# Five of the six sections of adaptive weights move from TensorE to ScalarE and GpSimd

## The chip, the cores and the metric

The kernel runs on one core of a Trainium2 chip. The metric is the device time of one execution in microseconds (us), the median of several runs. The engines of the core, as the profile names them, are PE (TensorE matmul) with PEld (its weight loads), DVE (VectorE), ACT (ScalarE), POOL (GpSimd) and SP (SyncE, which issues nearly all DMAs here). Each engine works off its own queue strictly in order.

## The reference

The program runs two blocks of a network over 256 tokens of width 1024, in float32. The first block has two layers, each steered by vectors that are computed from one conditioning vector `c`:

```python
silu_c = jax.nn.silu(c)                       # (1, 1024)
for i in range(DEPTH):                        # 2 layers
    mod = silu_c @ ada_w[i] + ada_b[i]        # (1, 6 * 1024)
    sh_t, sc_t, ga_t, sh_c, sc_c, ga_c = jnp.split(mod, 6, axis=-1)
    hn = modulate(rms_norm(x, norm_tm_g[i]), sh_t, sc_t)
    tm = rwkv7_mix(hn, ...) if i % 2 == 0 else dilated_attention_mix(hn, ...)
    x = x + ga_t[:, None, :] * tm
    ...                                       # mixture of experts, steered by sh_c, sc_c, ga_c
```

The change concerns `silu_c @ ada_w[i]` alone: a row of 1024 numbers times a 1024 x 6144 matrix, for two layers. The work that runs beside it is `rwkv7_mix` of layer 0, a recurrence over the tokens in two directions.

## The kernel before

The 2 x 6144 columns are cut into six sections of 2048 columns, one `Ada.steps(i, s)` each. A section reads 8 MB of weights in eight tiles of 1 MB, `[128 partitions, 2048 columns]`; partition p of tile k holds row 8 p + k of the matrix. TensorE takes a tile as the moving operand, in four column blocks j of 512, and `c[:, k]` (spread over 32 columns) as the weights, so that the four blocks land in four groups of 32 partitions of one PSUM bank. The eight k accumulate there. VectorE then adds the bias, and writes the section into the tiles `R`.

Section one is needed at once. The other five are a generator, `side`, that `rwkv` runs beside its own work; it yields after every k:

- `weave(preps(1, ...), every(side, 2))`: the second half of the preparation of the recurrence (decays, keys, scaled by VectorE, ScalarE and GpSimd). `kknorm` begins it; it sums squares on PE (L871), takes the root on ACT (L873) and goes on from there.
- `weave(inverses(), every(side, 2))`: the inverses of 16 x 16 triangular blocks, thirty dependent VectorE instructions (L1008, L1010) on `mcm`, which GpSimd clears first (L996, L998), transposed at the end by PE (L1015) and copied by ACT (L1017).
- `roundrobin([chain(0), chain(1), every(side, 3)])`: the recurrence, here called the chain. There are 16 jobs, eight in each direction, two at a time; a job starts with L1114 on PE, L1120 to L1124 on DVE and the transposition L1138 on PE, and ends with `across` (L1221 to L1241).

`every(gen, n)` lets n more turns pass after each step of `gen`. The final order on each engine is set by the tile scheduler, which merges the streams, so program order is only where it starts from.

Weight tiles come from a pool of four slots of 1 MB. In this stage some slots are held by others: `lb` until the last L894, `G` (a norm weight) during sections whose index s is 0 or 2, and `lg2` during the chain. A DMA into a slot waits until the last reader of the tile before is done.

Of the kernel before, what the change touches and what calls it, by code (L numbers as in the profile page):

```python
# [20 lines left out]
F32 = mybir.dt.float32  # L21
F32R = mybir.dt.float32r
I32 = mybir.dt.int32
AF = mybir.ActivationFunctionType
OP = mybir.AluOpType
AX = mybir.AxisListType
P = 128
# [3 lines left out]
KD = 8  # L31
# [550 lines left out]
def weave(main, *fill, rest=True):  # L582

    fill = [iter(f) for f in fill]
    for _ in main:
        while fill:
            try:
                next(fill[0])
                break
            except StopIteration:  # L590
                fill.pop(0)
    for f in fill if rest else ():
        finish(f)


def every(gen, n):

    for _ in gen:
        for _ in range(n):
            yield  # L600
# [104 lines left out]
def rwkv(N, src, I, cst, emit, side, tail, scratch):  # L705


    nc, tc = N.nc, N.tc
# [105 lines left out]
    def into_v(n):  # L814
# [4 lines left out]
            else:  # L819
                sc.activation(o, ps, AF.Copy)  # L820
        return ev
    side = iter(side)
    xk = shift_split(1, True)
    proj_fm(N, sp, *xk, wk, 0, into_fm(kf, 0))
    load_constants()
# [19 lines left out]
    ps = N.psum("b")  # L845
# [149 lines left out]
    def inverses():  # L995
        g.memset(mcm, 0.0)  # L996
        for c in range(16):
            g.memset(mcm[:, c, :, c:c + 1], 1.0)  # L998
        for t4 in range(4):
            ps = N.psum("b")  # L1000
            for t in range(4):
                nc.tensor.transpose(ps[0:64, t * P:(t + 1) * P], nd[:, 4 * t4 + t, :], N.ident)
            sc.activation(ncm[:, 4 * t4:4 * t4 + 4].rearrange("p t b i -> p (t b i)"), ps[0:64, :], AF.Copy)
        yield
        for k in range(15, 0, -1):
            n = 16 - k
            tv = tmp[:, 0:n * 8 * k].rearrange("p (c b i) -> p c b i", c=n, b=8)
            v.tensor_mul(tv, ncm[:, k:k + 1, :, 0:k].to_broadcast([64, n, 8, k]),  # L1008
                         mcm[:, k:, :, k:k + 1].to_broadcast([64, n, 8, k]))
            v.tensor_add(mcm[:, k:, :, 0:k], mcm[:, k:, :, 0:k], tv)  # L1010
            yield
        for h in range(2):
            ps = N.psum("b")
            for c in range(8):
                nc.tensor.transpose(ps[:, c * 64:(c + 1) * 64], mcm[:, 8 * h + c].rearrange("p b i -> p (b i)"),  # L1015
                                    N.ident[0:64, 0:64])
            sc.activation(m16[:, 8 * h:8 * h + 8], ps.rearrange("p (c x) -> p c x", c=8), AF.Copy)  # L1017
    m16 = pool("m16", 1, eM, "left").tile([P, 16, 64], F32, name="m16")
    weave(inverses(), every(side, 2), rest=False)
    e2s.close()  # L1020
    en.close()

# [223 lines left out]
    def chain(buf, jobs):  # L1246
        for z, et in jobs:
            yield from job(z, et, buf)
    late = []
    gens = [chain(0, [(0, et) for et in range(8)]), chain(1, [(1, et) for et in range(8)]), every(side, 3)]  # L1250
    roundrobin(gens)
    e4s.close()
    eM.close()
# [548 lines left out]
class Ada:  # L1802
# [34 lines left out]
    def steps(self, i, s):  # L1837
        N, I = self.N, self.I
        nc = N.nc
        v = nc.vector  # L1840
        S = self.np_.tile([P, 512], F32, name=N.nm("S"), tag="gt")
        b = I["ada_b"]
        nc.gpsimd.dma_start(S, bass.AP(tensor=b.tensor, offset=b.offset + i * 6144 + s * 2048,
                                       ap=[[512, 4], [0, 32], [1, 512]]))
        if s in (0, 2):
            gn = I["norm_tm_g" if s == 0 else "norm_cm_g"]
            h = slice(64, 128) if s == 0 else slice(0, 64)
            G = N.wp.tile([P, 2048], F32, name=N.nm("G"), tag="w")[:, 0:512]
            nc.gpsimd.dma_start(G[h], bass.AP(tensor=gn.tensor, offset=gn.offset + i * D, ap=[[512, 2], [0, 32], [1, 512]]))
        ps = N.psum("b")  # L1850
        w = I["ada_w"][i].rearrange("(p k) n -> p k n", k=KD)
        for k in range(KD):
            wt = N.wload(w[:, k, s * 2048:(s + 1) * 2048])
            for j in range(4):
                nc.tensor.matmul(ps[32 * j:32 * j + 32, :], self.c[:, k:k + 1].to_broadcast([P, 32]),  # L1855
                                 wt[:, j * 512:(j + 1) * 512], start=k == 0, stop=k == KD - 1)
            yield
        v.tensor_add(S, S, ps)
        if s in (0, 2):
            v.scalar_tensor_tensor(S[h], S[h], 1.0, G[h], op0=OP.add, op1=OP.mult)  # L1860
        q = 3 * i + s
        for k, r in enumerate(self.R):
            v.scalar_tensor_tensor(r, S, self.row[:, q:q + 1], r.bitcast(F32), op0=OP.mult, op1=OP.add)
            if k == 0:
                v.tensor_sub(S, S, r.bitcast(F32))
        yield
# [83 lines left out]
class Model:  # L1950
# [3 lines left out]
    def all(self):  # L1954
# [5 lines left out]
        with ExitStack() as es:  # L1960
# [28 lines left out]
            for i in range(2):  # L1989
                cm = {}  # L1990

                def emit(tt, n, ps):
                    xs = x[:, tt, HALVES[n]]
                    t = np_.tile([P, 512], F32, name=N.nm("gt"), tag="gt")
                    v.tensor_mul(t, ps, cm["ga"][n])
                    v.tensor_add(xs, xs, t)
                    cm["rms"].add(tt, n, xs, ps)
                    if n:
                        modulated(N, cm["rms"], tt, [x[:, tt, h] for h in HALVES], cm["A"], cm["B"], cm["h"][:, tt])

                if i == 0:
                    def side():
                        for q in range(1, 6):
                            yield from ada.steps(q // 3, q % 3)
                    mixer = rwkv(N, src, I, I["cst_rwkv"], emit, side(), tail, lambda k: half("G", k))
                else:
                    mixer = dilated(N, src, I, I["cst_attn"], emit, tail)
                next(mixer)
                cm["ga"] = gate(i, 2, "c")
                if i == 0:  # L2010
                    late = es.enter_context(tc.tile_pool(name="late", bufs=1))
                moe = Moe(N, I["moe_router_g"][i], I["moe_router_g_b"][i], I["moe_router_e"][i], I["moe_router_e_b"][i], True,
                          f(I["moe_w_gate"][i]), f(I["moe_w_up"][i]), f(I["moe_w_down"][i]))
                cm["rms"] = Rms(N, np_)
                cm["h"] = moe.xg_tile().rearrange("q k (t p) -> q t k p", t=NT)
                cm["B"], cm["A"] = ([ada.part(i, m, n, "c") for n in range(2)] for m in (3, 4))
                finish(mixer)
                N.open_extra(NEXTRA[1] + 2)
                moe.open()
                for tt in range(NT):  # L2020
                    moe.take(tt, cm["h"][:, tt])
                moe.scale = gate(i, 5)
                moe.route()
                nx = {}
                w = I["at_w_qkv"][0]

                def following(nx=nx, w=w):
                    AB = N.wtile("AB", own=True)
                    for j, (m, nm) in enumerate(((0, "B"), (1, "A"))):
                        nx[nm] = AB[:, j * D:(j + 1) * D]  # L2030
                        for n, h in enumerate(HALVES):
                            sc.activation(nx[nm][:, h], ada.part(1, m, n), AF.Copy)
                    N.prefetch(proj_srcs(w, 2048) + proj_srcs(w, 0)[:1], own=True)
                if i:
                    fg = halves("R")
                    for n, h in enumerate(HALVES):
                        nc.sync.dma_start(fg[n], I["final_g"][h].partition_broadcast(P))
                    ca = causal_setup(N, late)
                acc = moe.run(x, end=following if i == 0 else lambda: N.prefetch(mix_first(I, 0), own=True))
                rms = Rms(N, np_)  # L2040
                if i == 0:
                    def setup(tile, nx=nx):
                        nx["h"] = [tile(), tile()]

                    def norm(tt, acc=acc, rms=rms, nx=nx):
                        for n, h in enumerate(HALVES):
                            rms.add(tt, n, acc[tt, n], x[:, tt, h])
                        hk = nx["h"][tt].rearrange("q (k p) -> q k p", k=KD)
                        modulated(N, rms, tt, [acc[tt, n] for n in range(2)], *([nx[a][:, h] for h in HALVES] for a in "AB"), hk)
                        for n, h in enumerate(HALVES):  # L2050
                            sc.activation(x[:, tt, h], acc[tt, n], AF.Copy)
                    src = Source(norm, lambda tt, k, nx=nx: nx["h"][tt][:, k * P:(k + 1) * P], setup)
# [141 lines left out]
```

## Time and profile before

| what | us |
|---|---|
| median of 3 runs (2389.83 to 2395.27) | 2390.19 |
| the profiled execution, its own time | 2402.28 |
| its span in the trace | 2400.5 |
| PE busy / DVE busy / ACT busy / POOL busy | 2077.4 / 1154.3 / 707.3 / 366.4 |
| matmuls of the six sections (L1855), busy | 86.1 |

The span is the time between the first and the last instruction of the profiled execution. Busy times are unions over an engine's instructions; a PE that is busy need not be at its peak, since matmuls are pipelined and their ends are modelled. Idle time of an engine is written with what ended it. In this kernel the stretch that matters lies between 145 and 507 us of the span: 145 to 245 us preparation, 245 to 277 us inverses and the start of the first job, 277 to 507 us the chain.

### The profile page before, as it was taken

How to read it: one execution, taken by the hardware profiler on the slowest of the kernel's cores; microseconds unless marked ns; L12 is line 12 of the kernel's file. 1: busy time of each engine (PE TensorE's matmuls, PEld its weight loads, DVE VectorE, ACT ScalarE, POOL GpSimd, SP SyncE). 2: the span in 40 equal slices, each digit the busy share in tenths (PEclk: the TensorE clock that was granted, in tenths of full speed). 3: DMA queues.
4: the chain of work that ended last, by engine and by line, in shares of the span. 5: the costliest groups of instructions: out<-in, count | busy, mean ns of one | idle time of the engine just before them, and what ended most of it. 6: DMA issues, size and time to landing. Idle time of an engine off the chain costs nothing. (4 is left out here: it accounts for less than half of the span.)

```text
span 2400.5 us, 39938 instructions
## 1 busy us (share of the span) xinstructions
PE 2077.4 (87%) x16032; PEld 1482.2 (62%) x16032; DVE 1154.3 (48%) x2599; ACT 707.3 (29%) x1277; POOL 366.4 (15%) x300
## 2 busy tenths in 40 slices
PE   4987799897987799998997799989897799979895
PEld 2864366665653498997654377766564577766552
DVE  4777778774321435347331266563231575652132
ACT  2432244342110344434110234531120245421120
POOL 1144102231000221211000112220010222210010
PEclk7986799888998899999998899989998899989998
DMA  8424533156999663436999844477999544569996
GB/s 273 141 93 143 204 111 136 59 215 257 405 419 419 224 208 106 160 121 240 383 417 419 322 151 132 149 255 307 418 408 413 184 136 140 173 266 402 413 406 271
DMA packets 162994, 606.00 MB, mean 252 GB/s; under 512 B 36960, under 2 KB 37984, under 8 KB 107488
## 3 DMA queue, kind: packets, MB, share of 16 engines
q1 hardware_dynamic: 159072, 599.64, 65.9%
q0 software_dynamic: 3136, 3.16, 0.5%
q8 instruction: 132, 2.16, 0.4%
q10 hardware_dynamic: 576, 0.39, 0.1%
q14 instruction: 78, 0.64, 0.1%
HBM read 602.09 MB, written 1.05 MB: 251 GB/s over the span
## 5 line engine op out<-in xcount | busy, mean ns | idle before, releaser
L360 PE MATMUL psb<-w,xg 128*32 128x256 f32 (+1 forms) x4096 | 390.2, 427 | 88.4 <-DMA w<-in_moe_w_gate_dram 26.7
L360 PEld LDWEIGHTS psb<-w,xg 128*32 128x32 f32 (+1 forms) x4096 | 213.1, 133 | 274.0 <-issue 64.3
L562 ACT ACTIVATE wh<-w 128x1024 fp32r<-128x1024 f32 x230 | 240.6, 1060 | 291.1 <-PE psb L652 157.7
L566 POOL TENSOR_TENSOR wl<-w,wh 128x1024 fp32r<-128x1024 f32 x80 | 198.5, 2483 | 586.5 <-ACT wh L562 449.4
L566 DVE TENSOR_TENSOR wl<-w,wh 128x1024 fp32r<-128x1024 f32 x150 | 200.5, 1343 | 169.8 <-ACT wh L562 140.0
L420 DVE SCALAR_TENSOR_TENSOR hid<-psb,gs,sg 128x256 f32<-128x256 f32 x44 | 30.0, 682 | 394.4 <-PE psb L360 394.4
L651 PE MATMUL psb<-wh,xh 128*128 128x512 f32 x448 | 185.4, 415 | 4.0 <-ACT wh L562 2.4
L652 PE MATMUL psb<-wh,xl 128*128 128x512 f32 x448 | 181.5, 406 | 0.3 <-DVE xl L143 0.3
L360 PE MATMUL psb<-w,hT 128*32 128x512 f32 (+1 forms) x1024 | 173.3, 609 | 8.4 <-DMA w<-in_moe_w_down_dram 3.9
L649 PE MATMUL psb<-wl,xh 128*128 128x512 f32 x448 | 132.2, 403 | 3.2 <-POOL wl L566 1.7
L142 ACT ACTIVATE yh<-psb 128x512 fp32r<-128x512 f32 x88 | 52.5, 597 | 234.6 <-DVE psb L441 130.1
L1855 PE MATMUL psb<-w,c_fm 128*32 128x512 f32 x384 | 86.1, 779 | 35.1 <-DMA w<-in_ada_w_dram 29.5
L143 DVE TENSOR_TENSOR yl<-psb,yh 128x512 fp32r<-128x512 f32 x88 | 60.9, 692 | 104.7 <-ACT yh L142 104.7
L360 PEld LDWEIGHTS psb<-w,hT 128*32 128x32 f32 (+1 forms) x1024 | 50.7, 121 | 97.1 <-issue 70.8
L360 PE MATMUL psb<-pm,xh 128*128 128x256 f32 (+1 forms) x384 | 102.0, 302 | 4.3 <-DVE pm L343 3.2
L651 PEld LDWEIGHTS psb<-wh,xh 128*128 128x128 f32 x448 | 86.8, 194 | 24.3 <-ACT wh L562 3.6
L649 PEld LDWEIGHTS psb<-wl,xh 128*128 128x128 f32 x448 | 86.1, 194 | 23.4 <-POOL wl L566 2.5
L404 ACT ACTIVATE pt<-psb 128x256 fp32r<-128x256 f32 x44 | 16.9, 385 | 282.0 <-PE psb L360 282.0
L360 PE MATMUL psb<-pm,xl 128*128 128x256 f32 (+1 forms) x384 | 98.4, 292 | 0.0
L652 PEld LDWEIGHTS psb<-wh,xl 128*128 128x128 f32 x448 | 87.0, 194 | 18.4 <-DVE xl L143 1.2
L620 PE MATMUL psb<-axh,wh 128*128 128x256 f32 x384 | 93.7, 282 | 0.0
L620 PE MATMUL psb<-axl,wh 128*128 128x256 f32 x384 | 93.7, 282 | 0.0
(582 smaller groups left out, 3889.1 us busy)
## 6 DMA issues: line engine op xcount, KB each, us to landing
w<-in_moe_w_gate_dram SPq DMA_DIRECT2D x64, 1024.0 KB, 18.7
w<-in_moe_w_up_dram SPq DMA_DIRECT2D x64, 1024.0 KB, 18.5
w<-in_moe_w_down_dram SPq DMA_DIRECT2D x64, 1024.0 KB, 19.8
w<-in_w_exp_up_dram SPq DMA_DIRECT2D x64, 1024.0 KB, 13.2
w<-in_w_exp_gate_dram SPq DMA_DIRECT2D x64, 1024.0 KB, 10.3
w<-in_w_exp_down_dram SPq DMA_DIRECT2D x64, 1024.0 KB, 15.8
w<-in_ada_w_dram SPq DMA_DIRECT2D x48, 1024.0 KB, 5.1
w<-in_w_in_dram SPq DMA_DIRECT2D x44, 1024.0 KB, 5.1
```

Source lines behind the costliest of these rows:

```text
L142: self.nc.scalar.activation(hi, src, AF.Copy)
L143: (eng or self.nc.vector).tensor_sub(lo, src, hi.bitcast(F32))
L360: keep(nc.tensor.matmul(*a, **k))
L404: nc.scalar.activation(pt[g], ps[:, 0:256], AF.Copy)
L420: v.scalar_tensor_tensor(hid[g].rearrange("s j p -> s p j"), pu[:, :256].rearrange("s (p j) -> s p j", j=2), gs[g], sg.rearrange("s (p j) ...
L562: nc.scalar.activation(wh, w, AF.Copy)
L566: i = (nc.gpsimd if eng == "g" else nc.vector).tensor_sub(wl, w, wh.bitcast(F32))
L620: mm = lambda a, b, **f: nc.tensor.matmul(o, a[:, kk, ws], b[:, k, :], skip_group_check=True, **f)
L649: nc.tensor.matmul(pss[tt], xh[:, k, t], wl[:, kk, :], start=False, stop=k == nk - 1)
L651: nc.tensor.matmul(pss[tt], xh[:, k, t], wh[:, kk, :], start=k == 0, stop=False)
L652: nc.tensor.matmul(pss[tt], xl[:, k, t], wh[:, kk, :], start=False, stop=False)
L1855: nc.tensor.matmul(ps[32 * j:32 * j + 32, :], self.c[:, k:k + 1].to_broadcast([P, 32]), wt[:, j * 512:(j + 1) * 512], start=k == 0, stop=k ...
```

## The change

Section one stays as it was. In sections two to six a weight tile is now `[128, 4, 512]`: four k of one column block j. ScalarE multiplies each block of 512 columns in place by its per-partition number `c[:, k]`, GpSimd adds the eight products up into a tile `asum` in SBUF (seven additions), and TensorE sums `asum` over the partitions with one matmul against ones per j. The generator yields after two k, four times per column block, and no longer passes through `every`; the next weight tile is requested one ahead (`N.prefetch`). The new tile `asum` lies in the recurrence's pool `rp`, which is why `side` is now called with it.

```diff
-    side = iter(side)
+    side = iter(side(rp))
...
-    weave(inverses(), every(side, 2), rest=False)
+    weave(inverses(), side, rest=False)
...
-    gens = [chain(0, [(0, et) for et in range(8)]), chain(1, [(1, et) for et in range(8)]), every(side, 3)]
+    gens = [chain(0, [(0, et) for et in range(8)]), chain(1, [(1, et) for et in range(8)]), side]
...
-        for k in range(KD):
-            wt = N.wload(w[:, k, s * 2048:(s + 1) * 2048])
+        if i == s == 0:
+            for k in range(KD):
+                wt = N.wload(w[:, k, s * 2048:(s + 1) * 2048])
+                for j in range(4):
+                    nc.tensor.matmul(ps[32 * j:32 * j + 32, :], self.c[:, k:k + 1].to_broadcast([P, 32]),
+                                     wt[:, j * 512:(j + 1) * 512], start=k == 0, stop=k == KD - 1)
+                yield
+        else:
+            g = nc.gpsimd
+            srcs = [w[:, 4 * n:4 * n + 4, s * 2048 + j * 512:s * 2048 + (j + 1) * 512] for j in range(4) for n in range(2)]
             for j in range(4):
-                nc.tensor.matmul(ps[32 * j:32 * j + 32, :], self.c[:, k:k + 1].to_broadcast([P, 32]),
-                                 wt[:, j * 512:(j + 1) * 512], start=k == 0, stop=k == KD - 1)
-            yield
+                a = self.sums.tile([P, 512], F32, name=N.nm("asum"), tag="asum")
+                for k in range(KD):
+                    if k % 4 == 0:
+                        wt = N.wload(srcs[2 * j + k // 4])
+                        if k or j < 3:
+                            N.prefetch(srcs[2 * j + k // 4 + 1:][:1])
+                    u = wt[:, k % 4]
+                    sc.activation(u, u, AF.Copy, scale=self.c[:, k:k + 1])
+                    if k == 1:
+                        g.tensor_add(a, wt[:, 0], u)
+                    elif k:
+                        g.tensor_add(a, a, u)
+                    if k % 2:
+                        yield
+                nc.tensor.matmul(ps[32 * j:32 * j + 32, :], N.ones.bitcast(F32).to_broadcast([P, 32]), a, start=True, stop=True)
```

Counted over five sections: 160 matmuls go (two records each in the trace), 20 matmuls, 160 ScalarE instructions and 140 GpSimd instructions come; the 40 MB of weights are the same.

Three places in the queues show where the scheduler put the new work. The rows name line, operation, output<-input with buffer numbers, and shape; line numbers of the change are those of the changed kernel (L1870 the scaling, L1872 and L1874 the additions, L1877 the matmul with ones).

First, POOL at the end of the preparation, before: the last products `bk` of the preparation (L932), the clearing of `mcm` for the inverses, and the first job's `DP` stand together.

```order
L932 TENSOR_TENSOR bk_1403<-cu_1476,sg_1480 128x512
L912 COPY pl_836<-E_1551 128x8
L918 TENSOR_TENSOR ar_1402<-rf,E_1551 128x512
L932 TENSOR_TENSOR bk_1405<-cu_1485,sg_1489 128x512
L932 TENSOR_TENSOR bk_1404<-cu_1540,sg_1544 128x512
L932 TENSOR_TENSOR bk_1406<-cu_1549,sg_1553 128x512
L996 MEMSET mcm 64x2048
```

The same place of the change:

```order
L1872 TENSOR_TENSOR asum_1818<-w_1803 128x512
L1874 TENSOR_TENSOR asum_1818<-asum_1818,w_1803 128x512 x2
L1874 TENSOR_TENSOR asum_1818<-asum_1818,w_1830 128x512 x4
L932 TENSOR_TENSOR bk_1404<-cu_1538,sg_1542 128x512
L932 TENSOR_TENSOR bk_1406<-cu_1547,sg_1551 128x512
L1872 TENSOR_TENSOR asum_1856<-w_1857 128x512
L1874 TENSOR_TENSOR asum_1856<-asum_1856,w_1857 128x512 x2
L1874 TENSOR_TENSOR asum_1856<-asum_1856,w_1859 128x512 x2
L996 MEMSET mcm 64x2048
```

Between `aa_1499` (the last L901 but one of the preparation) and the clearing of `mcm` POOL now has 26 additions; 23 more follow up to the end of section three (`asum_2134`), which makes 49.

Second, PE around the first job's transposition L1138, before: it stands behind one matmul of section four.

```order
L1114 MATMUL psb_1968<-ar_839,bk_843 64x128 x2
L1855 MATMUL psb_1998<-w_1999,c_fm 32x512 [waits DMAHW5_49,DVE_49,PE_49]
L1855 MATMUL psb_1998<-w_1999,c_fm 32x512 x3
L1138 MATMUL psc_2010<-ident,MQB_1917 128x128 [waits DVE_49]
L1138 MATMUL psc_2010<-ident,MQB_1917 128x128 x3
```

In the change it stands behind the sum over the last column block of section three, which waits for GpSimd:

```order
L1114 MATMUL psb_2001<-ar_839,bk_843 64x128 [waits DVE_49,PE_49]
L1114 MATMUL psb_2001<-ar_839,bk_843 64x128 x7
L1877 MATMUL psb_1855<-asum_2134,ones 32x512 [waits Pool_49]
L1138 MATMUL psc_2036<-ident,MQB_1950 128x128 [waits DVE_49]
L1138 MATMUL psc_2036<-ident,MQB_1950 128x128 x3
```

So the first job cannot pass L1138 until GpSimd has finished all of section three.

Third, ACT before the root of `kknorm` (L873), before:

```order
L908 ACTIVATE sg_1284<-cu_1280 128x512 [waits Activation_49]
L820 ACTIVATE vt<-psb_1195 128x512 [waits PE_49]
L873 ACT_TABLE_LOAD
L873 ACTIVATE ri_1432<-psb_1427 8x256 [waits PE_49]
L897 ACT_TABLE_LOAD [waits PE_49]
```

The same place of the change has sixteen of the twenty scalings that now stand ahead of the root:

```order
L820 ACTIVATE vt<-psb_1195 128x512 [waits PE_49]
L1870 ACTIVATE w_1424<-w_1424,c_fm 128x512
L1870 ACTIVATE w_1492<-w_1492,c_fm 128x512 [waits DMAHW6_49,Pool_49]
L1870 ACTIVATE w_1492<-w_1492,c_fm 128x512 x3
L1870 ACTIVATE w_1600<-w_1600,c_fm 128x512 [waits DMAHW7_49,Pool_49]
L1870 ACTIVATE w_1600<-w_1600,c_fm 128x512 x3
L1870 ACTIVATE w_1695<-w_1695,c_fm 128x512 [waits DMAHW0_49,Pool_49]
L1870 ACTIVATE w_1695<-w_1695,c_fm 128x512 x3
L873 ACT_TABLE_LOAD
L873 ACTIVATE ri_1434<-psb_1429 8x256 [waits PE_49]
```

## Rows read from the trace of the kernel before

**Rows 1.** Page, busy us, share of the span and instructions of each engine.
```profile
PE 2077.4 (87%) x16032; PEld 1482.2 (62%) x16032; DVE 1154.3 (48%) x2599; ACT 707.3 (29%) x1277; POOL 366.4 (15%) x300
```

**Rows 2.** Windows: stretch, length, busy us of PE, PEld, DVE, ACT, POOL, clock, DMA.
```profile
205.00:245.00 40.00, 27.03 (x231) 17.29 (x234) 35.05 (x68) 8.18 (x17) 17.52 (x33) 0.66 0.38 127
245.00:277.00 32.00, 17.05 (x140) 6.37 (x132) 26.64 (x47) 1.20 (x2) 6.20 (x8) 0.68 0.73 258
277.00:507.00 230.00, 213.79 (x3367) 155.36 (x3367) 167.53 (x459) 95.23 (x275) 45.98 (x74) 0.95 0.32 109
```

**Rows 3.** The same windows, of L1855 alone: busy us of PE and PEld.
```profile
145.00:205.00 60.00, 10.20 (x36) 1.58 (x36) 0.74 0.35 123
277.00:507.00 230.00, 39.54 (x184) 5.52 (x184) 0.95 0.32 109
```

**Rows 4.** Timeline of PE, 225 to 300 us: start, us, instruction, idle before and releaser.
```profile
263.45 1.94 PE L1855 MATMUL psb<-w,c_fm 128*32 128x512 f32 x8 [3.15 <-DMA w<-in_ada_w_dram]
265.32 1.86 PE L1015 MATMUL psb<-ident,mcm 64*128 64x64 f32 x15
...
274.43 1.93 PE L1855 MATMUL psb<-w,c_fm 128*32 128x512 f32 x8 [3.83 <-issue]
277.02 1.12 PE L1138 MATMUL psc<-ident,MQB 128*128 128x128 f32 x4 [0.65 <-DVE MQB L1124]
...
287.66 1.04 PE L1855 MATMUL psb<-w,c_fm 128*32 128x512 f32 x2
```

**Rows 5.** Timeline of POOL, 180 to 300 us.
```profile
206.54 1.61 POOL L918 TENSOR_TENSOR ar<-rf,E 128x512 f32<-128x512 f32 x1
208.12 1.81 POOL L901 TENSOR_SCALAR aa<-aa 128x512 f32<-128x512 f32 x2
...
213.52 1.17 POOL L918 TENSOR_TENSOR ar<-rf,E 128x512 f32<-128x512 f32 x1
214.67 1.25 POOL L932 TENSOR_TENSOR bk<-cu,sg 128x512 f32<-128x512 f32 x1
...
216.09 1.17 POOL L918 TENSOR_TENSOR ar<-rf,E 128x512 f32<-128x512 f32 x1
```

**Rows 6.** Timeline of DVE, 180 to 300 us.
```profile
206.44 0.68 DVE L915 TENSOR_TENSOR ar<-kn,E 128x512 f32<-128x512 f32 x1
207.04 1.66 DVE L917 TENSOR_TENSOR bk<-bk,sg 128x512 f32<-128x512 f32 x1
...
213.42 3.99 DVE L929 TENSOR_SCALAR cu<-aa,pv 128x256 f32<-128x256 f32 x2
...
245.00 0.28 DVE L1008 TENSOR_TENSOR tmp<-ncm,mcm 64x120 f32<-64x120 f32 x1 [1.99 <-ACT ncm L1003]
...
261.65 0.35 DVE L1010 TENSOR_TENSOR mcm<-mcm,tmp 64x120 f32<-64x120 f32 x1
```

**Rows 7.** Timeline of ACT, 180 to 300 us.
```profile
188.63 0.37 ACT L873 ACTIVATE ri<-psb 8x256 f32<-8x256 f32 x1 [16.38 <-PE psb L871]
```

**Rows 8.** Groups of instructions, 120 to 240 us (ACT) and 277 to 507 us (others).
```profile
L908 ACT ACTIVATE sg<-cu 128x512 f32<-128x512 f32 x8 | 5.0, 622 | 0.0
L1078 POOL TENSOR_TENSOR G<-G,lw 128x512 f32<-128x512 f32 x6 | 7.6, 1269 | 0.6 <-DMA lw<-in_rw_ln_b_dram 0.2
L1124 DVE TENSOR_TENSOR MQB<-m,cm 128x512 f32<-128x512 f32 x15 | 16.0, 1095 | 5.0 <-PE psb L1187 5.0
L1130 DVE TENSOR_TENSOR bk<-bk,pl 128x256 f32<-128x256 f32 x16 | 8.1, 504 | 2.5 <-PE psb L1114 2.5
```

**Rows 9.** Waits, 277 to 507 us: who waited for whom, us in total, times, longest.
```profile
DVE ZZ L1151 <- PE psb L1149: 20.2, 17, 3.1
DVE MQB L1172 <- PE psb L1169: 18.0, 22, 1.8
```

**Rows 10.** DMA issues by line: KB each, median us from issue to landing.
```profile
w<-in_ada_w_dram SPq DMA_DIRECT2D x48, 1024.0 KB, 5.1
w<-in_rw_w_rkv_dram SPq DMA_DIRECT2D x12, 1024.0 KB, 5.7
```

More of the change, by code (lines that the diff above doesn't have):

```diff
@@ L1839, in steps @@
         nc = N.nc
-        v = nc.vector
+        v, sc = nc.vector, nc.scalar
         S = self.np_.tile([P, 512], F32, name=N.nm("S"), tag="gt")
@@ L2001, in all, with side @@
                 if i == 0:
-                    def side():
+                    def side(pool):
+                        ada.sums = pool
                         for q in range(1, 6):
                             yield from ada.steps(q // 3, q % 3)
-                    mixer = rwkv(N, src, I, I["cst_rwkv"], emit, side(), tail, lambda k: half("G", k))
+                    mixer = rwkv(N, src, I, I["cst_rwkv"], emit, side, tail, lambda k: half("G", k))
                 else:
```

## The prediction

> **What bounds the kernel now.** The first view is the table of engines. PE is busy 2077.4 of 2400.5 us (87%), POOL 366.4 (15%) [rows 1]. That is an average; the five sections run between 145 and 507 us, so the next view is the same table by stretch [rows 2]. Three stretches have different limits.
>
> From 205 to 245 us, the end of the preparation, DVE is busy 35.05 of 40 us and PE 27.03. From 245 to 277 us, the inverses, DVE has 26.64 of 32 and PE 17.05. In neither is PE the limit: DVE is, with POOL (17.52 of the first 40 us) feeding it. From 277 to 507 us, the chain, PE is busy 213.79 of 230 us (93%), DVE 167.53, ACT 95.23 and POOL 45.98. The list of waits of this stretch has DVE waiting for PE at the top, 20.2 us at L1151 and 18.0 us at L1172 [rows 9]. So PE leads there, though a recurrence also has a chain of its own, DVE to PE and back.
>
> L1855 costs PE 39.54 us in the chain (184 records) and 10.20 us between 145 and 205 us [rows 3]. The change can therefore give something back in the chain; in the stretches ahead of it TensorE has idle time, and VectorE and GpSimd, to which it adds, have the dependent work.
>
> **The prices.** A scaling on ACT has the shape of L908, 622 ns; an addition on POOL that of L1078, 1269 ns (one SBUF operand overwritten, the other from a weight tile) [rows 8]. A sum over the partitions, one column block alone in two records, took 1.04 us at full clock [rows 4]. The DMA of a weight tile with shorter rows is that of `in_rw_w_rkv`, 5.7 us instead of 5.1 [rows 10]: no difference by itself. Over five sections that is 160 x 0.62 = 99 us of ACT, 140 x 1.27 = 178 us of POOL, 20 x 1.04 = 21 us of PE.
>
> **(a) Preparation.** Before `kknorm`, PE no longer runs L1855 in 145 to 205 us. If all of it lay on the path that would be 10.2 us, if none, nothing; PE is not full there, and I take 4 us. Twenty scalings, 20 x 0.62 = 12.4 us, now stand ahead of the root L873 on ACT. They lie in the 16.38 us for which ACT idled there before, waiting for PE [rows 7], and so cost nothing; if a weight tile lands late or a slot comes free late, everything behind the root (`ri`, then the keys) moves by what is missing, up to 12 us.
>
> **(b) The start of the chain.** This is the largest term. The first job's transposition L1138 began at 277.02 us [rows 4]. In the change it stands on PE behind the sum over `asum_2134`, and PE works in order; so it cannot begin before POOL has done 49 additions that come after `aa_1499`. Before, `aa_1499` (the first of the two L901 at 208.12) ended at about 209.0 us [rows 5]; 4 us earlier by (a), 205. What else POOL does up to the chain is 17.52 + 6.20 us [rows 2], less the L918 of 1.61 and the half of L901 of 0.9 that are over by 209.0 [rows 5]: 21 us.
>
> The price of an addition beside DVE is not shown in the trace of before. Below, it is 1.27 us: 205 + 21 + 49 x 1.27 = 288, or +11 us. Above, it alternates each time with one DVE instruction of about the 0.68 us of L915 [rows 6], making 1.9: 205 + 21 + 93 = 319, or +42. The trace does show that the two engines hold each other up: L917 on DVE took 1.66 us beside POOL's L918, where L915, of the same shape and kind, took 0.68 [rows 6], and L929, two instructions, took 3.99 us during three POOL operations [rows 5, 6]. On the other side POOL's L918 took 1.61 us in that company and 1.17 us elsewhere [rows 5]. DVE is 83 to 88% busy here [rows 2], but a part of its work reads PSUM or one SBUF tile; I take half of the additions as meeting such an instruction, 1.55 us each: 205 + 21 + 76 = 302, **+25 us**.
>
> The Trainium skill, page "SBUF — State Buffer", section "Who interferes with whom", says that VectorE and GpSimd share a port pair under an exclusive lock, and that a VectorE operation with two SBUF inputs and a GpSimd operation that reads SBUF fully block each other. The trace agrees as far as L917's 1.66 against 0.68 us goes. By the rule taken to the full the sum would use the upper 319 us.
>
> DVE pays as well. The clearing of `mcm`, which opens the inverses (first L1008 at 245.00 us, last L1010 at 261.65 [rows 6]), is behind 26 of the 49 additions: 205 + 26 x 1.55 = 245, plus POOL's other work up to there, 21 less the 6.20 after 245 us, 15, is 260. The thirty short dependent instructions then take turns with additions: 16.65 us become at most 16.65 + 23 x 1.27 = 46. From 260 that ends between 277 and 306, so this second path arrives no later than the first by more than 4 us, and I count it once.
>
> **(c) The chain.** PE loses 39.54 us [rows 3] and gets 12 sums back, 12.5 us: 27 us less, 187 of some 225. ACT gets 96 scalings (60 us, to 155), POOL 84 additions (107 us, to 153) [rows 2, 8]; none of them is full. The gain lies between nothing and 27 us; as PE is 93% busy and DVE waits for it, nearer the upper end: 16 us. Against it, DVE's L1124 (1095 ns) and L1130 (504 ns) [rows 8] have two SBUF inputs and will meet additions: 16 jobs, at most one addition of 1.2 us each, 0 to 19 us; I take 8. Each sum makes PE wait for POOL's last addition, with the jobs' matmuls queued behind; 12 sums, at most one addition late each, 0 to 15 us. A tile is held for its DMA (5.7), four scalings (2.5) and four additions (5), 13 us, with two or three slots and a tile wanted each 225 / 24 = 9 us; that is just covered. For both I take 3. Net: -16 + 8 + 3 = **-5 us**, bounds -27 and +34.
>
> **The sum** is +25 - 5 = +20 us. The profiled execution took 2402.28 us, 12.1 above the median of 2390.19; I carry the difference, not the level: 2422 for a profiled execution, **2410 us** for the median.
>
> **The rivals.**
> A. PE's relief pays in full. POOL works at its alone price (+11), the chain gives the 27 us, locks and waits stay beside other work: -16, 2374 us. For it: 93% PE, 38 us of DVE waiting for PE [rows 2, 9]. Against it: the stretched L917 [rows 6]. It decides wherever the chain's gain passes the delay of L1138, so if an addition costs less than (27 - 21 + 72) / 49 = 1.59 us and the chain gives all (72 being 277 - 205).
> B. PE is not the limit. A matmul's busy time is no measure of a full PE: weight loads take 155.36 of the 230 us [rows 2], L1855 only 5.52 of these [rows 3], so that the chain's length may come from its dependences, and the relief is worth nothing. Then +25 + 8 + 3 = +36, 2426 us, with the upper start +53, 2443. The Trainium skill, "Perfetto Trace Analysis", section "Identifying the Most-Contended Engine", warns that matmul busy time is a bad measure and names weight-load busy time as a better one; by that the chain is at 68%.
> C. It cancels: start +11 us, relief 16, locks and waits 5; 2390 within 7 us.
>
> **The numbers.** The forecast (2397 to 2425) 0.47, A 0.25, B 0.14, C 0.14. Slower by over 0.3% (7 us, about what a measurement of this kernel can tell from no change) is the forecast and B, 0.61; same 0.14; faster 0.25. The range 2373 to 2440 leaves out B's upper part and the part of A in which (a) gives more than 4 us.
>
> **What would show it.** (a): L873 begins at about 185 us, not later than 188.6. (b): the first L1138 begins near 302 us, PE waiting at L1877 for POOL just ahead; POOL's additions average 1.5 to 1.6 us between 205 and 302; first L1008 near 260 and the inverses well over 16.65 us. (c): from the first L1138 to the end of the chain some 225 us instead of 230, with L1124 longer than 1.1 us and PE's busy time about 187. Wrong if L1138 begins before 288 (then A or C), if L873 comes later than 190 because ACT waits for weights (then slower than forecast), or if the chain shrinks by over 20 us or grows.

## The result, and the profile after

The changed kernel takes 2507.95 us (2504.49 to 2509.91, 4 runs) beside 2392.73 us of the kernel before in the same runs: ratio 1.0472, 95% interval 1.0452 to 1.0493, slower by 115 us. The prediction was 2410 us with a range up to 2440: the sign held, the size did not.

Engine table of the page, as in [rows 1]:

```profile
PE 2064.9 (82%) x15752; PEld 1489.6 (59%) x15752; DVE 1215.3 (48%) x2599; ACT 803.8 (32%) x1437; POOL 561.3 (22%) x440
```

Over the whole program PE is relieved by 12.5 us only. Where the time went is read from two marks that both kernels have: the first L1138, with which the first job gets going, and the last L1241, with which the last job ends (I call the time between them the chain from here on). The views of line L1241, before and after, give shortest, median and longest duration, then first and last start:

```profile
L1241 ACT ACTIVATE bk<-psc x8: 377/384/386, 435.3 to 513.7; 128x256 f32<-128x256 f32 x8
```

```profile
L1241 ACT ACTIVATE bk<-psc x8: 378/383/384, 534.1 to 628.3; 128x256 f32<-128x256 f32 x8
```

The chain ends 114.6 us later, which is the 115 us of the medians. (The spans of these two executions differ by 107.6 us only: behind the chain, where both kernels have the same work, that of before took 1886.8 us and that of the change 1879.8.) PE's timeline of the change shows the start, where [rows 4] had L1138 at 277.02:

```profile
297.27 1.92 PE L1877 MATMUL psb<-asum,ones 128*32 128x512 f32 x2 [11.67 <-POOL asum L1874]
302.81 1.86 PE L1015 MATMUL psb<-ident,mcm 64*128 64x64 f32 x15 [3.62 <-DVE mcm L1010]
304.60 3.68 PE L1114 MATMUL psb<-ar,bk 64*64 64x128 f32 x48
308.57 1.97 PE L1114 MATMUL psb<-ar,bk 64*64 64x128 f32 x16 [0.29 <-DVE LGK L1122]
315.43 1.91 PE L1877 MATMUL psb<-asum,ones 128*32 128x512 f32 x2 [4.89 <-POOL asum L1874]
317.27 1.12 PE L1138 MATMUL psc<-ident,MQB 128*128 128x128 f32 x4
```

So L1138 comes 40.3 us later, right behind the last sum of section three, and the chain is 311.0 us long instead of 236.7, another 74.3. The windows answer to [rows 2], with the chain between its two marks as the third row; the row of the kernel before for its own marks follows:

```profile
205.00:245.00 40.00, 11.95 (x130) 6.39 (x134) 39.42 (x45) 13.93 (x26) 33.46 (x27) 0.56 0.29 92
245.00:277.00 32.00, 11.31 (x73) 7.32 (x65) 21.52 (x32) 12.54 (x21) 29.55 (x39) 0.61 0.48 161
317.30:628.30 311.00, 223.14 (x3230) 175.11 (x3230) 194.09 (x472) 155.05 (x380) 162.20 (x160) 0.81 0.32 104
```

```profile
277.00:513.70 236.70, 219.23 (x3390) 158.69 (x3391) 173.05 (x478) 97.99 (x285) 46.22 (x75) 0.95 0.34 114
```

Two things stand out. Ahead of the chain POOL and DVE are both nearly full. In the chain nobody is: PE is busy 223 of 311 us, DVE 194, ACT 155, POOL 162. The chain has become long by waiting. Six of the longest waits in it (as in [rows 9], but all engines), and below them PE's wait at L1114 before:

```profile
PEld psb L1114 <- ACT YH L1211: 37.4, 13, 11.1
PE psb L1114 <- ACT YH L1211: 34.4, 11, 10.8
PEld psb L1877 <- POOL asum L1874: 31.3, 5, 8.1
PE psb L1877 <- POOL asum L1874: 30.3, 5, 7.9
ACT w L1870 <- DMA w<-in_ada_w_dram: 30.3, 12, 6.5
DVE MQB L1172 <- PE psb L1169: 27.1, 24, 9.6
```

```profile
PE psb L1114 <- ACT YH L1211: 6.5, 9, 1.9
```

PE stands 30.3 us at the sums for GpSimd, and 34.4 us at L1114 for a copy on ACT (6.5 us before); ACT stands 30.3 us in its own queue for weights. Why the weights are late shows in SP's queue, which issues their loads (L78): a load stands there until the last reader of its slot is done. The longest of these waits from 140 us to the end of the chain, before and after (microseconds in total, times, longest):

```profile
SPq L78 <- PE psb L1855: 152.6, 23, 24.4
```

```profile
SPq L78 <- POOL asum L1874: 314.6, 34, 21.0
```

Before, the slots came back from TensorE (another 121.9 us of waits end with its L1227); now they come back when GpSimd has added. What makes GpSimd late makes the weights late.

How the additions and VectorE treat each other shows best in the inverses, thirty dependent VectorE instructions with two SBUF inputs. Line L1008, before and after:

```profile
L1008 DVE TENSOR_TENSOR tmp<-ncm,mcm x15: 277/550/683, 245.0 to 261.3; 64x120 f32<-64x120 f32 x2, 64x224 f32<-64x224 f32 x2, 64x312 f32<-64x312 f32 x2, 64x384 f32<-64x384 f32 x2
```

```profile
L1008 DVE TENSOR_TENSOR tmp<-ncm,mcm x15: 383/1497/1635, 268.2 to 301.1; 64x120 f32<-64x120 f32 x2, 64x224 f32<-64x224 f32 x2, 64x312 f32<-64x312 f32 x2, 64x384 f32<-64x384 f32 x2
```

The median goes from 550 to 1497 ns, and the inverses from 17 to 34.5 us; VectorE ran nothing but these thirty instructions in them. GpSimd pays too. Its groups from 211 us (where `aa_1499` is done) to 315 us, and the window with PE, PEld, DVE, ACT and POOL:

```profile
L1874 POOL TENSOR_TENSOR asum<-asum,w 128x512 f32<-128x512 f32 x42 | 59.7, 1421 | 2.7
L1872 POOL TENSOR_TENSOR asum<-w 128x512 f32<-128x512 f32 x7 | 9.7, 1385 | 9.9 <-PE psb L1877 4.2 <-issue 3.6 <-ACT w L1870 2.1
...
211.00:315.00 104.00, 32.27 (x240) 19.92 (x240) 91.30 (x113) 33.81 (x56) 90.28 (x86) 0.53 0.35 117
```

These are the 49 additions of the prediction's step (b), at 1.42 us each. GpSimd is busy 90 of 104 us, and 9.9 of its 14 idle us stand in front of the first addition of a column block (L1872).

### The profile page after: what moved, and what is told of

Read it like the earlier page. It is cut to its first block, busy times and chain, and to the rows that moved or that the text cites. A ratio compares the mean times of both kernels' runs of the same rounds, so it can differ in the third digit from the quotient of the medians.

```text
span 2508.1 us, 39784 instructions
## 1 busy us (share of the span) xinstructions
PE 2064.9 (82%) x15752; PEld 1489.6 (59%) x15752; DVE 1215.3 (48%) x2599; ACT 803.8 (32%) x1437; POOL 561.3 (22%) x440
## 5 line engine op out<-in xcount | busy, mean ns | idle before, releaser
L360 PE MATMUL psb<-w,xg 128*32 128x256 f32 (+1 forms) x4096 | 397.0, 437 | 86.4 <-DMA w<-in_moe_w_up_dram 26.5
L360 PE MATMUL psb<-w,hT 128*32 128x512 f32 (+1 forms) x1024 | 167.4, 597 | 6.7 <-DMA w<-in_moe_w_down_dram 4.6
L1874 POOL TENSOR_TENSOR asum<-asum,w 128x512 f32<-128x512 f32 x120 | 167.9, 1399 | 11.4 <-ACT w L1870 3.7
L1870 ACT ACTIVATE w<-w,c_fm 128x512 f32<-128x512 f32 x160 | 104.9, 714 | 87.1 <-DMA w<-in_ada_w_dram 86.6
L1911 POOL TENSOR_TENSOR rst<-rst,mhalf 128x1 f32<-128x1 f32 x10 | 6.2, 624 | 536.7 <-DMA G<-in_ln_g_dram 243.3
L1877 PE MATMUL psb<-asum,ones 128*32 128x512 f32 x40 | 32.7, 913 | 96.3 <-POOL asum L1874 96.2
```

Of the source, the lines that this page charges most:

```text
L360: keep(nc.tensor.matmul(*a, **k))
L1870: sc.activation(u, u, AF.Copy, scale=self.c[:, k:k + 1])
L1874: g.tensor_add(a, a, u)
L1877: nc.tensor.matmul(ps[32 * j:32 * j + 32, :], N.ones.bitcast(F32).to_broadcast([P, 32]), a, start=True, stop=True)
```

## The experiments

All start from the changed kernel unless said. Starts and lengths are of the profiled executions; the median is in us, the ratio is to the kernel before, with its 95% interval. A mark is read from one execution: relief, which changes nothing ahead of the chain, starts 3.9 us earlier than before, and prep_only has before's code in the chain and takes 5.1 us less for it, so differences of some 5 us between marks say nothing. Where part of the sums is left out, the program goes on with other values, and later stages take another time (up to 3233 us in total, with a chain that differs by 20 us): of those runs the two marks count, not the total.

| run | first L1138 | chain | median, ratio |
|---|---|---|---|
| before | 277.0 | 236.7 | |
| the change | 317.3 | 311.0 | 2507.95, 1.0472 (1.0452 to 1.0493) |
| chain_only | 271.1 | 309.9 | 2462.03, 1.0292 (1.0257 to 1.0326) |
| prep_only | 317.2 | 231.6 | 2435.65, 1.0175 (1.0146 to 1.0205) |
| two_sums | 308.9 | 299.8 | 2491.81, 1.0401 (1.0373 to 1.0429) |
| late_sums | 310.2 | 308.9 | 2498.37, 1.0432 (1.0403 to 1.0460) |
| no_loads | 316.5 | 290.4 | part left out |
| no_loads_late | 308.1 | 291.0 | part left out |
| one_add | 278.2 | 251.1 | part left out |
| memsets | 284.3 | 277.6 | part left out |
| memsets_late | 285.1 | 266.6 | part left out |
| dve_fused | 297.0 | 292.4 | 2468.69, 1.0327 (1.0291 to 1.0362) |
| pace1_prep (from before) | 284.0 | 240.8 | 2408.19, 1.0060 (1.0041 to 1.0080) |
| relief (from before) | 273.1 | 226.7 | part left out |

**Two stages, each by itself.** chain_only and prep_only keep the old form in the other sections, with two or three turns per k, as many as `every` gave:

```diff
-        if i == s == 0:
+        q0 = 3 * i + s
+        if q0 < 3:                # chain_only; prep_only: if q0 == 0 or q0 > 2
...
-                yield
+                for _ in range(2 if q0 else 1):      # prep_only: 3
+                    yield
```

chain_only: 

> Sections two and three are summed on TensorE as before; only sections four to six, in the chain, have the new form. The change cost 40 us up to the first L1138 (317.3 against 277.0) and 74 us from there to the end of the chain. Theory A (the two stages are slowed apart, each by its own loop of scaling, additions and sum): first L1138 back near 277 us, chain still about 300 us long, about 40 us faster than the full change, near 2468 us. Theory B (the chain is slow because it starts with a backlog, with slots and GpSimd late): the chain shortens too, to under 260 us, total below 2430 us.

prep_only: 

> Sections two and three have the new form; four to six, in the chain, are summed on TensorE as before. Theory A: first L1138 near 317 us and the chain back near 230 us, total near 2432 us. Theory B: as the start is late, the chain stays some 20 us or more longer than 230 us, total above 2450 us.

Theory A held in both. With the new form in the chain alone, the start is at 271.1 and the chain 309.9; with it in the preparation alone, the start is at 317.2 and the chain 231.6, as if nothing had happened. The delays of 65 and 38 us add up to 103 of the 115. A backlog (B) is excluded.

**One buffer of asum, and the sum in PE's queue.** two_sums takes a second buffer from the chain's pool `p4` (ahead of the chain there is no room for one); late_sums also issues each sum after five scalings of the next block:

```diff
+    sums.append(p4)
...
-                a = self.sums.tile([P, 512], F32, name=N.nm("asum"), tag="asum")
+                a = self.sums[j % len(self.sums)].tile([P, 512], F32, name=N.nm("asum"), tag="asum")
...
+                    if k == 4 and late_sum:      # late_sums
+                        sum_up(*late_sum)
```

two_sums: 

> The full change with two buffers for asum during the chain instead of one. Theory A1 (GpSimd waits 40.6 us in the chain for the sum on TensorE to release the only asum, and this paces the loop): these waits go and the chain shortens by 20 to 40 us, total 2470 to 2490 us. Theory A2 (the loop is paced by weight tiles, which come late because a slot is held until GpSimd's last addition of it): within 8 us of the full change, 2500 to 2515 us. Theory A3 (TensorE standing in order at the sum paces the chain): a few us only, since the sum still stands where it stood.

late_sums: 

> As with two asum buffers in the chain, and there each sum over the partitions is issued five scalings of the next column block later, so that TensorE meets it when it is long ready. Theory A3: TensorE's waits at the sum (30 us in the chain) go, and the chain shortens by 30 us or more, total at or below 2475 us. Theory A2: at most 10 us beyond what two buffers gave, because the weights still come late and ScalarE stands in order before its scalings.

Two buffers give the chain 11 us, less than A1 wanted. Late sums on top of them take 9 of these back, so that the two together give 2 us: A3 fails as the main cause. PE's wait at the sums did fall, from 17.7 us in the chain of two_sums to 8.2 in that of late_sums, but its wait for ACT's copy at L1114 rose from 23.6 to 49.8, and ACT stood 47.7 us for weights (45.0 in two_sums): the wait moved. In two_sums and late_sums the scheduler also put seven instead of eight sums ahead of the first L1138, and the start came at 309 or 310 us instead of 317.3: L1138 then follows L1114 and VectorE's L1124, and so the inverses, without a sum between.

**Late weights.**

```diff
-                        wt = N.wload(srcs[2 * j + k // 4])
-                        if k or j < 3:
-                            N.prefetch(srcs[2 * j + k // 4 + 1:][:1])
+                        if i == 0:
...
+                        else:
+                            if j == 0:
+                                kept[k // 4] = N.wload(srcs[k // 4])
+                            wt = kept[k // 4]
```

no_loads: 

> The full change, but in sections four to six the two weight tiles of the first column block serve all four, so 18 of 24 loads of the chain are left out (and the values of these sections with them). Theory A2 (late weights hold ScalarE in order, and ScalarE the chain): ScalarE's 30 us of waits for weights go and the chain, 303 us long, shortens by 30 us or more, total at or below 2475 us. Theory A4 (the chain is stretched by the work and the in-order sums as such): the chain shortens by under 12 us, total 2495 to 2510 us.

no_loads_late: 

> The same left out, together with two buffers of asum in the chain and the sum over the partitions issued five scalings later. If the chain is stretched by three waits alone (weights, asum, TensorE at the sum), it comes to 235 to 250 us and the total to 2430 to 2450 us, the 40 us of the start remaining. If the scalings themselves (96 of 0.71 us in ScalarE's queue ahead of the chain's own copies) and the additions stretch it, the chain stays above 265 us and the total above 2465 us.

no_loads shortens the chain by 20.6 us, between what A2 and A4 said. PE's waits in no_loads (the sum is L1883 there):

```profile
PE psb L1883 <- POOL asum L1880: 33.5, 6, 8.0
PE psb L1114 <- ACT YH L1211: 18.6, 12, 2.6
```

PE's wait for ACT's copy falls from 34.4 to 18.6 us: late weights do hold ACT in order, and ACT holds the chain. The wait for GpSimd's sum stays. Taking most of it away as well (12.1 us are left in no_loads_late) brought nothing more, 291.0 us; there ACT met another wait, 21.4 us for GpSimd to have read the block it is to scale again. Removing waits one by one moves the chain by 2 to 21 us, as another wait takes the place. The waits for a slot, for asum, for the sum and for the block to scale have GpSimd's additions behind them, so these were taken away next.

**The additions, and what in them.** one_add drops the additions from k = 2 on; memsets replaces those of k = 2 to 6 by clearings of the tile, which read nothing:

```diff
-                    elif k:                      # one_add: both lines go
+                    elif k == 7:
                         g.tensor_add(a, a, u)
+                    elif k:
+                        g.memset(wt[:, 0:k % 4 + 1], 0.0)
```

one_add: 

> The full change with only the first addition of each column block: 120 of 140 additions are left out (and the sums with them). Theory of the start: the inverses, 34.5 us beside additions, go back to about 17 us, and the first L1138 to 280 to 287 us. Theory A (the loop runs through GpSimd's additions): slots come free after the scaling, and the chain shortens to under 260 us; total 2400 to 2435 us. If ScalarE's scalings and the loads were the cost, the chain stays above 285 us and the total above 2460 us.

memsets: 

> The full change with 100 of the 140 additions replaced by clearings of the weight tile that take GpSimd about as long on average but read nothing (the sums are wrong by what is left out). If additions hurt by locking VectorE out, the inverses go from 34.5 to under 20 us, the first L1138 comes 10 to 17 us earlier, and in the chain VectorE's 20 us more of busy time go and the chain shortens by 10 to 20 us. If GpSimd's time and the order in which queues wait for it are what hurts, the inverses alone shorten, the first L1138 still waits for GpSimd near 315 us, and the chain stays above 300 us.

memsets_late: 

> The same clearings in place of additions, with two buffers of asum and later sums in the chain. If lock and TensorE's wait at the sum together make the chain long, it comes below 270 us; if the late weights and GpSimd's time do, it stays above 285 us.

Without 120 additions the start is back (278.2) and the chain is 59.9 us shorter, 251.1: the additions are 39 of the 40 us of the start and 60 of the 74 us of the chain. All 160 scalings and all loads are still there and cost, less the relief of PE, the remaining 14 us. The expected 17 us for the inverses did not come: they took 28.0 us, at a median of 601 ns for L1008, since VectorE worked off the end of a section between them and stood 6.1 us in order for its sum.

With clearings, GpSimd is busy 157.6 us in the chain (162.2 with additions), but the start is at 284.3 and the chain 33 us shorter. So it is not GpSimd's time that costs these 33 us: the start did not stay near 315 us, nor the chain above 300. The sizes differ from the expected ones: the inverses, with two of seven additions left, take 22.5 us and not under 20, and start and chain gain more than expected. DVE's timeline in the inverses of memsets shows what a clearing spares VectorE:

```profile
256.35 1.97 DVE L1010 TENSOR_TENSOR mcm<-mcm,tmp 64x440 f32<-64x440 f32 x1
258.35 0.65 DVE L1008 TENSOR_TENSOR tmp<-ncm,mcm 64x480 f32<-64x480 f32 x1
259.04 2.99 DVE L1010 TENSOR_TENSOR mcm<-mcm,tmp 64x480 f32<-64x480 f32 x1
262.06 0.68 DVE L1008 TENSOR_TENSOR tmp<-ncm,mcm 64x504 f32<-64x504 f32 x1
```

And POOL's at the same time:

```profile
256.55 1.29 POOL L1874 TENSOR_TENSOR asum<-asum,w 128x512 f32<-128x512 f32 x1
257.76 1.40 POOL L1876 MEMSET w<- 128x1536 f32 x1
259.10 1.20 POOL L1133 TENSOR_TENSOR DP<-cm,pl 128x256 f32<-128x256 f32 x2
260.24 1.26 POOL L1872 TENSOR_TENSOR asum<-w 128x512 f32<-128x512 f32 x1
261.57 1.38 POOL L1876 MEMSET w<- 128x1536 f32 x1
```

Beside a clearing VectorE takes its own 0.65 us, beside an addition 1.97, beside three reading operations 2.99. PE's wait at the sum in the chain, 30.3 us with additions, is 5.6 here (the sum is L1879; window 290 to 545 us):

```profile
PE psb L1114 <- ACT YH L1211: 26.2, 12, 4.9
PE psb L1149 <- ACT Mt L1142: 10.5, 8, 3.1
PE psb L1879 <- POOL asum L1874: 5.6, 3, 2.3
```

The comparison is not quite pure: seven sums stand ahead of L1138 here too, and one more in the chain than in the change, so for the start two_sums is the fair partner, and the share of the lock, by which VectorE and GpSimd shut each other out, is 308.9 - 284.3 = 25 us. For memsets_late it is late_sums: the chain goes from 308.9 to 266.6, below the 270 us at which lock and the wait at the sum together were to be the answer.

**The relief of PE alone.** From the kernel before; relief leaves out six of eight k of L1855 in the chain, pace1_prep only changes the pace:

```diff
-            for j in range(4):
+            for j in range(4) if i == 0 or k in (0, KD - 1) else ():
```

```diff
-    weave(inverses(), every(side, 2), rest=False)      # and the same for preps(1)
+    weave(inverses(), every(side, 1), rest=False)
```

relief: 

> The kernel before, with six of the eight k of sections four to six left out on TensorE (their weights are loaded, their values are missing from the sums): the relief of TensorE without any of the work that takes its place. L1855 costs TensorE 40 us in the chain before, here about 10. The prediction's step (c) gives the chain about 18 us of these 30; if TensorE's work does not bound the chain (rival B), it stays within 5 us of 237 us. Since later work depends on the values, the stretch up to the chain's end is what counts, not the total.

pace1_prep: 

> The kernel before, all sums on TensorE, with one turn instead of two after each step of the sections in the preparation and the inverses, so that more of the sections lies where TensorE has idle time (44.1 of 72 us busy from 205 to 277 us) and less in the chain. If TensorE's work bounds the chain, as the prediction took it, the chain shortens by up to the part of the 39.5 us that moves ahead, some 5 to 20 us. If it does not, or if slots keep the loads from coming earlier, within 5 us of before.

The chain of relief, all engines and then L1855 alone:

```profile
273.10:499.80 226.70, 194.01 (x3245) 157.75 (x3246) 173.97 (x479) 97.69 (x284) 45.67 (x75) 0.92 0.39 132
```

```profile
273.10:499.80 226.70, 7.40 (x40) 1.04 (x40) 0.92 0.39 132
```

PE is relieved of 32.6 us and the chain shortens by 10.0. Some of that may be no relief: prep_only has the chain's code of before and takes 231.6 us for it, so between 5 and 10 us, at most a third of the 32.6, are the relief's. The median fits: 2380.64 us beside 2389.11, 8.5 us less with the start in it. In pace1_prep L1855's 40 us in the chain became 18.8, the chain did not shorten at all (240.8), as expected for work that does not bound it, and the start moved 7 us back. So what the change could ever have won in the chain is, by estimate, at most some 7 us (a third of the 22 by which it relieves PE).

**VectorE instead of ScalarE and GpSimd.**

```diff
-            g = nc.gpsimd
+            g = nc.vector
...
-                    sc.activation(u, u, AF.Copy, scale=self.c[:, k:k + 1])
-                    if k == 1:
...
+                    if k == 0:
+                        g.tensor_scalar(a, u, self.c[:, k:k + 1], None, op0=OP.mult)
+                    else:
+                        g.scalar_tensor_tensor(a, u, self.c[:, k:k + 1], a, op0=OP.mult, op1=OP.add)
```

dve_fused: 

> The full change, but VectorE alone scales and adds, one instruction for each k (160 of about 0.7 us, 96 of them in the chain); ScalarE and GpSimd have none of it, and nothing locks. If the waits of ScalarE, GpSimd and the lock made the loss, most of it goes: first L1138 by 290 us, total 2400 to 2440 us, with VectorE's 67 us more in the chain as the remaining cost. If the wait of TensorE for each sum in order was the loss, it stays above 2470 us.

Most of the loss stayed: 80 us over the 2389.11 us of before in these runs, where the change has 115. No addition on POOL and no scaling on ACT is involved, but the start is at 297.0, since DVE is the limit there, and in the chain DVE is busy 246.5 of 292.4 us. The expected 2400 to 2440 us and the start by 290 were missed: the start comes 20.0 us later than before, and the chain is 55.7 us longer, with VectorE busy 73.5 us more in it; this work too stands in one queue with the jobs' own. The total is near the 2470 us of the other expectation, but not for its reason: PE waits 6.3 us at the sums in this chain, not 30. No run that does all the work beats the kernel before.

## Why the prediction was wrong

Of the 115 us, the start has 40 where the prediction had 25, and the chain 74 where it had -5. That the sum had the right sign is owed to the start; in the chain, which makes two thirds of the loss, the prediction had the sign wrong.

**(a) Preparation: no 4 us.** ACT's timeline at the root, to be read with [rows 7]:

```profile
181.65 2.56 ACT L1870 ACTIVATE w<-w,c_fm 128x512 f32<-128x512 f32 x4 [5.23 <-DMA w<-in_ada_w_dram]
184.23 1.28 ACT L873 ACT_TABLE_LOAD   x1
190.04 0.37 ACT L873 ACTIVATE ri<-psb 8x256 f32<-8x256 f32 x1 [4.53 <-PE psb L871]
```

The cover held: the twenty scalings are over at 184.2 and ACT still waits 4.53 us for PE. But the root comes at 190.0 instead of 188.6, not at 185. PE's place was taken by waits for DVE, between 145 and 192 us before and after:

```profile
PE psb L949 <- DVE aa L943: 6.9, 4, 4.9
...
PE psc L925 <- DVE bk L917: 1.4, 1, 1.4
```

```profile
PE psb L949 <- DVE aa L943: 9.7, 5, 6.9
PE psc L925 <- DVE bk L917: 3.8, 2, 3.4
```

PE was not the limit there, and DVE had become slower: from 145 us to the root 51 instructions before had it busy for 27.9 us, and 50 in the change for 32.2.

**(b) The start: the right places, +40.3 for +25.** Both paths that the prediction named arrived within 7 us of each other: the inverses, with which PE would have been ready at about 310.5 (end of L1114), and the 49 additions with their sum at 317.3. The price of an addition, 1.55 us, was even too high (1.42 measured). What failed is that the additions were added up as if they stood end to end: `aa_1499` was done at 211, not 205, and POOL idled 14 us between them, mostly at block boundaries, where the single asum waits for its sum on PE, or the next block for its scalings. With 21 us of other work, as predicted, and 69 of additions that makes 315, and the sum itself, which the prediction had left out here, another 1.9. The inverses came out at 34.5 us, inside the bound of 46, but began at 268.2, not 260. The upper bound of 319 us, which was also what the sum gave by the rule of the Trainium skill ("SBUF — State Buffer", section "Who interferes with whom"), was the better forecast, though by 1.42 us for an addition plus idle time, not by 1.9.

**(c) The chain: +74.3 for -5, outside the bounds of -27 and +34.** Three terms of it were wrong.
- The relief, 16 us, is the term that rival B attacked. At most a third of a relief arrives (relief), so the 22 us net would be 7 at most. In the change even that is gone: apart from L1855 and the sums, PE's matmuls are busy 223.14 - 17.7 = 205 us where before they were 219.23 - 40.0 = 179. The granted clock of the chain is 0.81 instead of 0.95; behind its waits PE runs at the lower of its two levels (the sum took 1.91 us at 315.43 after 4.89 us of idleness, at a granted clock of 0.53 from 211 to 315 us; 1.04 at full clock in [rows 4]). What the lower clock itself adds to the chain no run separates.
- The lock, 8 us, was counted for L1124 and L1130 and once per job. Rows of the change's chain show whom it hits, against [rows 8]: a mean of 1257 and 654 ns where it was 1095 and 504, which is 4.5 us for the two lines, and an instruction that reads PSUM, unchanged (its row of before stands last):

```profile
L1120 DVE TENSOR_TENSOR MQB<-psb,cm 64x256 f32<-64x256 f32 x56 | 23.6, 421 | 13.3 <-PE psb L1114 12.4
...
L1124 DVE TENSOR_TENSOR MQB<-m,cm 128x512 f32<-128x512 f32 x14 | 17.3, 1257 | 5.7 <-PE psb L1187 5.7
...
L1130 DVE TENSOR_TENSOR bk<-bk,pl 128x256 f32<-128x256 f32 x15 | 9.8, 654 | 14.3 <-PE psb L1114 14.3
```

```profile
L1120 DVE TENSOR_TENSOR MQB<-psb,cm 64x256 f32<-64x256 f32 x60 | 25.3, 421 | 3.0 <-PE psb L1114 1.9
```

 DVE's busy time grows by 21 us in all (173.05 to 194.09), some 4 of them for six more instructions of the sections' ends that now fall into the chain. Taking the reading out of 100 additions, 60 of them those of sections four to six, gave the chain 33 us (memsets), with 10 us less of DVE's busy time (183.87). So the lock was mis-sized because it was priced by the instructions that it lengthens; most of what it costs came as waits in other queues, such as PE's at the sums. By which of them is not shown.
- The waits, 3 us, were judged from averages: 13 us to hold a tile, 9 us between tiles, "just covered". They came to 30.3 us of ACT for weights and 30.3 us of PE for sums, up to 7.9 at a time, and what stands behind them in order (YH, then L1114) to another 28. These waits overlap and do not add up to the loss. GpSimd's own time and place in this loop is 60 - 33 = 27 us of the chain, the part of one_add that memsets did not give. So the 74 us are 33 for the additions' reading, 27 for GpSimd's time and place, and 14 for scalings and loads, less the relief.

How these 27 us divide between weight slots, the single asum and GpSimd's own part of the jobs stays open: with additions, the waits removed gave 2 to 21 us, and the gains did not add up; with clearings, the second buffer and late sums together gave 11 us (277.6 to 266.6).

The change did start where the prediction said, and rival A (relief in full) and C (it cancels) are excluded by relief and one_add: even with 120 additions left out, the chain is 14 us longer than before. Rival B was near the truth about the relief, but its 2426 to 2443 us missed the result as well, with the same 8 and 3 us for lock and waits.

## What to carry to other kernels

Work moved to an idle engine is not free if that engine's instructions stand between others' in order: price the loop (load, scaling, additions, sum, release), with its single buffers, against the stretch's pace, and not its busy time against the idle time. Before paying for a relief, leave the relieved work out and time it: here 32.6 us of TensorE's busy time were worth 10 at most. Additions on GpSimd belong beside VectorE work that reads PSUM, not beside a dependent sequence with two SBUF inputs.

## What the runs showed of the hardware

- GpSimd's additions slow VectorE's two-SBUF-input instructions nearly threefold in a dense sequence (550 to 1497 ns median), do not touch those with a PSUM input (421 and 421 ns), and clearings on GpSimd do not slow even the former (0.65 us beside one). The Trainium skill, "SBUF — State Buffer", section "Who interferes with whom", says just this of operations that only write; the traces agree. The price to GpSimd is smaller: 1.27 to 1.42 us an addition between 211 and 315 us.
- The busy time of TensorE in a stretch is no fixed sum of its work: with 70 us more of idleness between them, the same matmuls showed 26 us more of busy time in the chain (205 for 179), at a granted clock of 0.81 for 0.95.
